# State-space tables from factors that are transposed once, complex products of three, and each batch's outputs directly in front of the next batch's products

## The chip, the core and the metric

The kernel runs on one core of a Trainium2 chip. The metric is the device time of one execution in microseconds (us); the time of a kernel is the median of its runs. The core has five engines that follow streams of instructions of their own: TensorE (PE) multiplies matrices and its weight loads (PEld) run beside the products, VectorE (DVE), ScalarE (ACT) and GpSimd (POOL) work on tiles element by element, and SyncE (SP) only issues DMA transfers. ACT and POOL can issue transfers too. Semaphores join the streams.

## What is computed

The input is a sequence of 1024 frames of 1024 channels in fp32. Layer 0 projects it to an S5 state-space branch and a retention branch, each with a SiLU gate, and maps both back; layer 1 is a gated convolution module. The change lies in the state-space branch, cut here to what matters:

```python
mag = exp(a_re * dt)                               # 64 groups x 64 states
lb  = mag * (cos(a_im * dt), sin(a_im * dt))       # complex decay of a step
bb  = coef(lb, a) * (b_re, b_im)                   # 64 groups x 64 states x 16 inputs
bu  = einsum('tbgh,gnh->tbgn', u, bb)              # inputs into the states
x   = associative_scan(lb, bu)                     # x[t] = lb * x[t-1] + bu[t]
y   = einsum(x_re, c_re) - einsum(x_im, c_im) + dsk * u
y   = gelu(y); y = y * sigmoid(y @ glu_w + glu_b)
```

## The kernel before

**Products of three.** A dense product takes three matmuls, high by high part, low by high, high by low (`mm3`, L276 to L278), each with 128x128 weights and 512 columns. A block of 128 output channels over the whole sequence is 2 halves x 8 x 3 = 48 matmuls.

**The first stage** is `layer0_front` (L337). It makes eight blocks `u` of the branch's input (`mm_u`; evacuated at L443, stored as `u_d` at L451), while DVE, ACT and POOL compute the state-space parameters (`s5_params`: powers `pr`, `pi` of the decay, phases `e1`, `e2`, and the factors `bbr`, `bbi`). Then come sixteen gate blocks (`mm_g`, nb 8 to 23), in pairs. During each pair one of eight *batches* B of the state-space layer is done, 128 channels each: 8 groups of 16, which are 4 pairs q of 2 groups with 128 states. Time is cut into 128 steps m of 8 frames j.

**A batch.** POOL makes three complex tables as outer products of the parameters (`s5_tables`, `outer`, six operations of 128x512 each): `Mr, Mi` (bb times the power j), the rotations `Tc, Ts`, and `W3` (c times the power j + 1). ACT makes `R8` (decay over 8 frames). `s5_states` then

- transposes Mr and Mi on PE in eight matmuls (`w2r`, `w2i`, L837), and ACT copies the two banks to `W2`;
- multiplies U, the batch's part of `u_d`, by W2 (`v`, L848), and DVE rotates and scans v into the states `S` (L856 to L876);
- makes the kernel matrix of a step: `kp` (L882, L883, eight matmuls of `cbr`, `cbni`, which are c set out in blocks by the host, with Mr and Mi), copied to `Kg` by ACT, with the skip `dd` added into its first 16 columns by DVE (L886), transposed on PE (`kt`, L888), copied to `Kt`, stored as one transfer into `k_d` (L892), read back as `Wd` in Toeplitz form (L895), and copied to `W1` (L897).

`s5_out(B)` makes the outputs of the batch: sixteen matmuls `y<-U,W` with W1 (L912) and thirty-two `y<-S,W` with W3 (L918), which ACT copies to `yb`, stored as `y_d` (L924). It is called for batch B - 1 after the first gate block of pair B.

**What sets the order.** Each engine runs its stream in order. A scheduler writes the streams from the program's dependencies with a timeline of its own and takes what comes earlier in the code first. It may set later independent instructions into a gap, which is why the same pieces stand at different distances in different batches. `issue_after` holds an instruction back behind another one, and `chained` keeps a list together. SP issues nearly all transfers, each in its place in SP's stream: the loads and stores of the batches, of the gates (`gs_d`, `gr_d`, L462) and of the *weight sums* (`weight_sums`, L244 to L254: rows `a` of another weight are loaded, added on DVE and stored as `ws`), which fill DVE and the transfers from nb 13 to nb 20. *Input sums* of the same kind follow in nb 9 to 12, held behind `last_kg`, the DVE operation at L886.

## Time and profile before

| | |
|---|---|
| median of 3 runs | 1179.47 us (1176.72 to 1180.49) |
| span of the profiled execution (its own time is not listed apart) | 1173.9 us |
| ACT busy | 545.1 us (46%), 821 instructions |
| transfers | 270.66 MB, mean 231 GB/s |
| Wd<-k_d, U<-u_d, y_d<-yb: 512 KB each, from issue to landing | 5.1, 4.6, 4.8 us |
| wf_g<-w_ab (weights of a gate block, 512 KB) | 5.4 us |
| first transpose w2 of batch 0 | 100.90 us after the span's start |

How such rows are read: a row of the timeline has the start in us, the length, the engine, the line of the code, the operation and its tiles (result <- operands), the shape, and the number of instructions put together in the row. `128*64 128x128` on PE is the shape of the weights and that of the moving operand. `SPq` is a transfer issued by SP. A square bracket tells how long the engine had been idle ahead of the row, and what ended that. A row of the waits has the engine and tile that waited, what it waited for, the sum in us, the count and the longest. A row of the windows has the window and its length, then for PE, DVE, ACT, POOL and PEld the busy time and the count of instructions, the granted clock, the share of the DMA engines that was busy, and GB/s.

### The profile page before, as it was taken

What the parts mean: (1) busy time and instruction counts of PE and PEld (TensorE: products, weight loads), DVE (VectorE), ACT (ScalarE), POOL (GpSimd) and SP (SyncE); (2) the same over time, 40 slices, a digit from 0 to 9 for tenths busy, and PEclk for the clock granted to TensorE, in tenths of its full rate; (3) what the DMA queues carried; (4) which work ended last, traced back from release to release, by engine and by line L of the source; (5) the groups of instructions that cost most, each with busy time, mean ns of one, the idle gap of its engine ahead of it and who ended that gap; (6) DMA issues with size and microseconds to landing.
All of it is one profiled execution on the core that took longest, in us unless ns stands there. A gap on an engine that the chain in (4) does not pass through costs nothing.

```text
span 1173.9 us, 17492 instructions
## 1 busy us (share of the span) xinstructions
PE 1161.3 (99%) x6150; PEld 965.5 (82%) x6150; DVE 910.5 (78%) x1507; ACT 545.1 (46%) x821; POOL 713.5 (61%) x507
## 2 busy tenths in 40 slices
PE   9999999999999999999999999999999999999997
PEld 7888888888888888887788888888888888888887
DVE  7875789999717475689777888479999999999643
ACT  7212343332226642123645544367756678544662
POOL 2049999888843245664444034348894689977742
PEclk9999999999999999999999999999999999999999
DMA  9353378778789765765988468965448553357863
GB/s 344 109 178 109 134 270 312 272 269 282 273 307 325 268 228 192 251 190 180 362 313 304 160 220 268 309 232 188 161 158 306 216 182 132 134 176 243 281 247 138
DMA packets 131192, 270.66 MB, mean 231 GB/s; under 512 B 12832, under 2 KB 41760, under 8 KB 130976
## 3 DMA queue, kind: packets, MB, share of 16 engines
q1 hardware_dynamic: 129952, 265.35, 66.5%
q10 hardware_dynamic: 1152, 4.19, 0.9%
q8 instruction: 48, 0.79, 0.3%
q14 instruction: 40, 0.33, 0.1%
HBM read 193.54 MB, written 71.76 MB: 226 GB/s over the span
## 4 chain that ended last, share of the span: by engine, by line
PE 91%; DMA 4%; DVE 2%; SPq 1%; ACT 1%; POOL 1%; issue 1%; DVEq 0%; POOLq 0%; ACTq 0%
PE mm_g L277 8%; PE mm_g L278 8%; PE mm_g L276 7%; PE mm_w L278 4%; PE mm_w L277 4%; PE mm_w L276 4%; PE mm_a L278 2%; PE mm_b L277 2%; PE mm_a L276 2%; PE mm_b L278 2%; PE mm_a L277 2%; PE mm_b L276 2%; PE mm_u L278 2%; PE mm_oc L278 2%; PE mm_u L277 2%; PE mm_oc L277 2%
## 5 line engine op out<-in xcount | busy, mean ns | idle before, releaser
L1461 DVE SCALAR_TENSOR_TENSOR cv<-u,convw,cv 128x512 f32<-128x512 f32 x358 | 244.7, 750 | 5.0 <-ACT cv L1447 3.5
L1441 POOL TENSOR_TENSOR tp<-tp,tp 128x512 f32<-128x512 f32 x104 | 138.9, 1338 | 28.7 <-ACT tp L1440 23.4
L278 PE MATMUL mm_g<-xh,wl_g 128*128 128x512 f32 x256 | 100.8, 394 | 0.0
L277 PE MATMUL mm_g<-xl,wh_g 128*128 128x512 f32 x256 | 100.7, 394 | 0.0
L276 PE MATMUL mm_g<-xh,wh_g 128*128 128x512 f32 x256 | 100.5, 393 | 0.0
L1440 ACT ACTIVATE tp<-u,convw 128x512 f32<-128x512 f32 x104 | 69.6, 713 | 9.6 <-POOL tp L1441 9.4
L277 PEld LDWEIGHTS mm_g<-xl,wh_g 128*128 128x128 f32 x256 | 48.1, 188 | 11.2 <-issue 1.6
L278 PEld LDWEIGHTS mm_g<-xh,wl_g 128*128 128x128 f32 x256 | 48.0, 188 | 10.5
L276 PEld LDWEIGHTS mm_g<-xh,wh_g 128*128 128x128 f32 x256 | 48.1, 188 | 9.6
L278 PE MATMUL mm_oc<-zh,wl_woc 128*128 128x512 f32 (+1 forms) x152 | 54.5, 360 | 0.2 <-DMA wl_woc<-lo_woc 0.2
L276 PE MATMUL mm_oc<-zh,wh_woc 128*128 128x512 f32 (+1 forms) x152 | 54.3, 362 | 0.0
L277 PE MATMUL mm_oc<-zl,wh_woc 128*128 128x512 f32 (+1 forms) x152 | 54.0, 357 | 0.0
L276 PE MATMUL mm_glu<-yh,wh_glu 128*128 128x512 f32 x128 | 50.0, 392 | 1.3 <-ACT sg L1250 1.3
L277 PE MATMUL mm_u<-xl,wh_u 128*128 128x512 f32 x128 | 50.1, 391 | 1.0 <-DVE xl L390 0.9
L276 PE MATMUL mm_g<-h1h,wh_cg 128*128 128x512 f32 x128 | 50.3, 393 | 0.0
L276 PE MATMUL mm_a<-h1h,wh_ca 128*128 128x512 f32 x128 | 50.3, 393 | 0.0
L278 PE MATMUL mm_b<-h1h,wl_cb 128*128 128x512 f32 x128 | 50.3, 393 | 0.0
L232 ACT CAST lh<-lf 128x512 fp32r<-128x512 f32 x32 | 19.5, 618 | 65.9 <-DMA lf<-w_c 59.3
L278 PE MATMUL mm_a<-h1h,wl_ca 128*128 128x512 f32 x128 | 50.0, 391 | 0.0
L277 PE MATMUL mm_glu<-yl,wh_glu 128*128 128x512 f32 x128 | 50.0, 392 | 0.0
L278 PE MATMUL mm_g<-h1h,wl_cg 128*128 128x512 f32 x128 | 49.9, 390 | 0.0
L277 PE MATMUL mm_g<-h1l,wh_cg 128*128 128x512 f32 x128 | 49.9, 390 | 0.0
(811 smaller groups left out, 3637.3 us busy)
## 6 DMA issues: line engine op xcount, KB each, us to landing
wf_g<-w_ab SPq DMA_DIRECT2D x16, 512.0 KB, 5.4
a<-w_out SPq DMA_DIRECT2D x32, 256.0 KB, 4.4
ws<-a SPq DMA_DIRECT2D x32, 256.0 KB, 4.8
lf<-w_c SPq DMA_DIRECT2D x32, 256.0 KB, 5.3
wf_p<-ws SPq DMA_DIRECT2D x16, 512.0 KB, 4.1
wf_cb<-w_c SPq DMA_DIRECT2D x16, 512.0 KB, 4.9
wf_ca<-w_c SPq DMA_DIRECT2D x16, 512.0 KB, 4.7
wl_cb<-lo_cb SPq DMA_DIRECT2D x16, 512.0 KB, 3.4
```

The costliest lines, as they stand in the source:

```text
L232: self.nc.scalar.copy(hi[:], f[:])
L276: nc.tensor.matmul(ps, wh[:, kb, :], xh, start=start, stop=False)
L277: nc.tensor.matmul(ps, wh[:, kb, :], xl, start=False, stop=False)
L278: self.last_mm = nc.tensor.matmul(ps, wl[:, kb, :], xh, start=False, stop=stop)
L1440: nc.scalar.mul(sk[:], u[:, k:k + HALF], cw[:, nb, k:k + 1])
L1441: gp.tensor_tensor(s0[:], s0[:], sk[:], op=ALU.add)
L1461: v.scalar_tensor_tensor(dst[:], *tap, accs_[i][:], op0=ALU.mult, op1=ALU.add)
```

## The change

Nothing changes in what the kernel computes. In the code:

- **Factors transposed once.** `bbr`, `bbi` are written with the inputs h ahead of q. After the first half of block u6, `s5_turned` transposes them and the powers in twelve matmuls (`turn_p`, `turn_br`, `turn_bi`); ACT copies the three banks and issues the stores to `pt_d` and `bt_d`, and copies the factors into `bblk`, set out in blocks of 32 columns. The host's `s5_cbr`, `s5_cbi` and their loads go, and the blocks u5 and u6 are now called ahead of the change of pools.
- **W2 without transposes.** Per batch, four transfers of 256 KB read `PT`, `BT` with repeats (from SP; for batch 0 from ACT), and POOL multiplies them in six operations directly into `W2`.
- **Complex products of three.** `Tc, Ts` and `W3` are made by `outer3`, five operations in place of six, from the sums and differences `psum`, `e1s`, `e2s`, `e1i` (now with e1r taken off), `cdif`, `csum`, which are made once.
- **The kernel matrix from W3.** W3 has nine times 16 columns; the first 16 are c itself, copied by ACT. kp is the product of W3 with `bblk`, which gives it in the transposed form, so that `kt` and `Kt` go. The skip is added on PE by four matmuls of the identity with 16 columns of `dd`, in place of the DVE operation. k_d is stored from ACT in eight transfers of runs of 64 bytes.
- **Order.** `s5_out(B - 1)` is called ahead of `s5_states(B)`, in front of the gate blocks. The input sums wait for the last write of S in place of `last_kg`. The stores of `y_d` and of the gates go from SP to ACT. The load of U is called in `s5_tables`, one gate block earlier. `tmpP`, `R8` have one buffer, `tmpV` two.

The first place is PE's stream around batch 3. Names carry the batch (`v_3`, `y_2`) and the scheduler's own number; `mm_g` are gate matmuls. Before, batch 3 is met in three pieces with gate matmuls between them:

```order
L837 MATMUL w2r_1928<-ident,Mr_1872 128x128 x4
L837 MATMUL w2i_1935<-ident,Mi_1873 128x128 x4
L276 MATMUL mm_g_0_2008<-xh_0_134,wh_g_1701 128x512
...
L848 MATMUL v_3_1942<-U_1926,W2r_1933 64x128 x8
L848 MATMUL v_3_1951<-U_1926,W2i_1940 64x128 x8
L882 MATMUL kp_1980<-Mr_1872,s_s_cbr 32x128
L883 MATMUL kp_1980<-Mi_1873,s_s_cbi 32x128
...
L888 MATMUL kt_1992<-ident,Kg_1989 128x128
L912 MATMUL y_2_2064<-U_1615,W_2_1688 128x128
L912 MATMUL y_2_2065<-U_1615,W_2_1688 128x128
...
L918 MATMUL y_2_2064<-S_1659,W_2_1577 128x128
L918 MATMUL y_2_2065<-S_1659,W_2_1577 128x128
```

After, the same place is one piece. Of the 48 matmuls y_2 the last four are shown:

```order
L973 MATMUL y_2_1972<-S_1720,W_2_1624 128x128
L973 MATMUL y_2_1973<-S_1720,W_2_1624 128x128
L973 MATMUL y_2_1972<-S_1720,W_2_1624 128x128
L973 MATMUL y_2_1973<-S_1720,W_2_1624 128x128
L904 MATMUL v_3_2001<-U_1944,W2r_1919 64x128 x8
L904 MATMUL v_3_2010<-U_1944,W2i_1920 64x128 x8
L937 MATMUL kp_2039<-W_3_1921,s_bblkr 32x128 x4
L939 MATMUL kp_2039<-s_s_dd,ident 32x16 x4
L940 MATMUL kp_2039<-W_3_1921,s_bblki 32x128 x4
L276 MATMUL mm_g_0_2073<-xh_0_134,wh_g_1768 128x512
L277 MATMUL mm_g_0_2073<-xl_0_135,wh_g_1768 128x512
```

The outputs y_2 have moved from behind the first gate block to the place right ahead of v_3; w2 and kt are gone, and the diagonal with `s_s_dd` stands between the two halves of kp. The batches 1 to 7 all look so, with 96 gate matmuls between one and the next. Batch 0 stands apart: its v in two parts and its kp in two lie among gate matmuls, and behind its last kp come 65 gate matmuls and then y_0.

The second place is PE's stream at the first half of block u6, which had only `mm_u` there before. The twelve transposes now stand between its two halves (`mm_u_0`, `mm_u_1`):

```order
L278 MATMUL mm_u_0_927<-xh_0_214,wl_u_803 128x512
L806 MATMUL turn_p<-ident,s_pr 128x128 x2
L806 MATMUL turn_p<-ident,s_pi 128x128 x2
L806 MATMUL turn_br<-ident,s_bbr 128x128 x4
L806 MATMUL turn_bi<-ident,s_bbi 128x128 x4
L276 MATMUL mm_u_1_986<-xh_1_142,wh_u_802 128x512
L277 MATMUL mm_u_1_986<-xl_1_143,wh_u_802 128x512
```

They are 72 matmuls `mm_u` ahead of the first gate matmul. Nothing of them is in the batches any more.

The third place is SP's stream between the outputs of batch 2 and the W1 of batch 3. Before (weight sums `a`, `ws` all around):

```order
L892 DMA k_d<-Kt_1994 128x128
L830 DMA U_2225<-u_d 128x1024
L895 DMA Wd_1997<-k_d 128x8x128
L462 DMA gs_d<-gt_2007 128x1024
L254 DMA ws_0_1914<-a_1_2095 128x512
L265 DMA wf_g_2599<-w_ab 128x1024
```

After, at the load of the same Wd (the number after its name is the scheduler's):

```order
L868 DMA PTr_2505<-ptr 128x1x512
L871 DMA BTi_2508<-bti 128x1x512
L244 DMA a_2_2252<-w_out 128x512
...
L868 DMA PTi_2506<-pti 128x1x512
L871 DMA BTr_2507<-btr 128x1x512
L950 DMA Wd_2062<-k_d 128x8x128
L254 DMA ws_0_1959<-a_1_2130 128x512
```

The store of k_d and that of the gate have left SP, and four loads PT, BT of batch 5 stand a few rows ahead of the load of Wd of batch 3. The stores are now in ACT's stream, with SiLUs (`gt`), a weight cast (`wh_g`), `R` and the two copies of c (`W`) between them:

```order
L977 COPY yb_1971<-y_2_1972 128x4x128
L977 COPY yb_1971<-y_2_1973 128x4x128
L878 COPY W_4_2218<-s_s_cr 128x4x16
L878 COPY W_4_2218<-s_s_ci 128x4x16
L979 DMA y_d<-yb_1971 128x1024
L944 COPY Kg_2052<-kp_2039 128x128
L947 DMA k_d<-Kg_2052 16x8x16 x8
L886 ACTIVATE R_4_2243<-s_s_m_480,s_r_614 128x128 x4
L462 ACTIVATE gt_2072<-gt_2072 128x512
L267 CAST wh_g_2145<-wf_g_2144 128x1024
L462 ACTIVATE gt_2072<-gt_2072 128x512
L465 DMA gs_d<-gt_2072 128x1024
```

In ACT's stream of batch 3 there stand now, between the copy of yb and that of W1, the store of y_d, the copy of Kg, eight stores of k_d and one of a gate.

The diff, cut to its core:

```diff
...
@@ -443,6 +443,9 @@
                 self.u_evac[nb] = nc.vector.tensor_tensor(
                     ut[:, ::-1, h * 64:(h + 1) * 64], ps[:].rearrange("p (m j) -> p j m", j=8),
                     r.rearrange("p (m j) -> p j m", j=8), op=ALU.mult)
+                if (nb, h) == (6, 0):
+                    with tc.issue_after(self.last_mm.ins):
+                        self.s5_turned(ev)
...
-            nc.sync.dma_start(dst[k * P:(k + 1) * P], gt[:])
+            nc.scalar.dma_start(dst[k * P:(k + 1) * P], gt[:])
...
+        for nb in (5, 6):
+            u_block(nb)
         early.close()
         sums = self.pool("sums", 1, stack=st)
         self.s5 = self.pool("s5w", 1, stack=st)
-        for nb in range(5, 8):
-            u_block(nb)
+        u_block(7)
         self.s5_tab, self.s5_back, self.s5_last = {}, {}, None
         self.s5_tables(0)
         for nb in range(8, 24):
             B = (nb - 8) // 2
             if nb % 2 == 0:
+                if B:
+                    self.s5_out(B - 1)
                 self.s5_states(B)
                 if nb in (10, 12):
-                    with self.tc.issue_after(self.last_kg.ins):
+                    with self.tc.issue_after(self.last_s.ins):
...
-            if nb % 2 == 0 and B:
-                self.s5_out(B - 1)
...
-        self.cbr, self.cbni = load("s5_cbr", (NP, 32)), load("s5_cbi", (NP, 32))
+        self.bblk = [sp.tile([P, NP, 32], F32, name=f"s5_bblk{c}") for c in "ri"]
+        for b in self.bblk:
+            nc.gpsimd.memset(b[:], 0.0)
...
+        self.psum = t((9, NP), keep="s5_psum")
+        tt(self.psum[:], pr_[:], pi_[:], ALU.add)
+        self.cdif, self.csum = t((NP, 16), keep="s5_cdif"), t((NP, 16), keep="s5_csum")
...
+        self.e2s = t((8, NP), keep="s5_e2s")
+        self.e1s = t((17, NP), keep="s5_e1s")
+        tt(self.e2s[:], e2r[:], e2i[:], ALU.add)
+        tt(self.e1s[:], e1r[:], e1i[:], ALU.add)
+        self.last_phase = tt(e1i[:], e1i[:], e1r[:], ALU.subtract)
...
-        self.bbr, self.bbi = t((NP, 16), keep="s5_bbr"), t((NP, 16), keep="s5_bbi")
+        self.bbr, self.bbi = (tp.tile([P, 16, NP], F32, name=f"s5_bb{c}") for c in "ri")
...
+        tt(self.cdif[:], self.cr[:], self.nci[:], ALU.add, gp)
+        tt(self.csum[:], self.cr[:], self.nci[:], ALU.subtract, gp)
...
-        tt(self.bbr[:], x1[0], x1[1], ALU.subtract, gp)
-        tt(self.bbi[:], x1[2], x1[3], ALU.add, gp)
+        tt(self.bbr[:].rearrange("p h q -> p q h"), x1[0], x1[1], ALU.subtract, gp)
+        tt(self.bbi[:].rearrange("p h q -> p q h"), x1[2], x1[3], ALU.add, gp)
+    def s5_turned(self, tp):
+        nc = self.nc
+        self.pt_d = [self.dram.tile([8, 32, P], F32, name=f"pt{c}") for c in "ri"]
+        self.bt_d = [self.dram.tile([16, 32, P], F32, name=f"bt{c}") for c in "ri"]
+        def turn(name, srcs, dsts):
+            ps = self.bank(f"turn_{name}")
+            for i, src in enumerate(srcs):
+                nc.tensor.transpose(ps[:, i * P:(i + 1) * P], src, self.ident[:])
+            t = tp.tile([P, 8, P], F32, name=f"turned_{name}", tag="xin", bufs=8)[:, :4, :]
+            self.last_turn = nc.scalar.copy(t.rearrange("p i n -> p (i n)"), ps[:])
+            n = len(srcs) // len(dsts)
+            for i, dst in enumerate(dsts):
+                nc.scalar.dma_start(dst.rearrange("(i p) n -> p i n", p=P), t[:, i * n:(i + 1) * n, :])
+        fl = lambda t: t.rearrange("p a b -> p (a b)")
+        cols = lambda t, n: [fl(t)[:, i * P:(i + 1) * P] for i in range(n)]
+        rows = lambda d: d[:].rearrange("a b n -> (a b) n")
+        turn("p", cols(self.pr[:, 0:8, :], 2) + cols(self.pi[:, 0:8, :], 2), [rows(d) for d in self.pt_d])
+        for c, b in zip("ri", (self.bbr, self.bbi)):
+            turn(f"b{c}", cols(b[:], 4), [rows(self.bt_d["ri".index(c)])])
+        for blk, b in zip(self.bblk, (self.bbr, self.bbi)):
+            for g in range(2):
+                r = slice(64 * g, 64 * g + 64)
+                with self.tc.issue_after(self.last_turn.ins):
+                    nc.scalar.copy(blk[r, :, 16 * g:16 * g + 16], b[r].rearrange("p h q -> p q h"))
...
+    def outer3(self, B, o_r, o_i, k1, k2, k3, view, op_i):
+        gp = self.nc.gpsimd
+        t = self.big(f"o_{B}", "tmpP", 1)
+        yield gp.tensor_tensor(view(t[:]), *k1, op=ALU.mult)
+        yield gp.tensor_tensor(view(o_r), *k3, op=ALU.mult)
+        yield gp.tensor_tensor(o_r, t[:], o_r, op=ALU.subtract)
+        yield gp.tensor_tensor(view(o_i), *k2, op=ALU.mult)
+        yield gp.tensor_tensor(o_i, o_i, t[:], op=op_i)
...
-        made = [self.outer(B, Mr[:], Mi[:], bj(self.bbr), bj(self.bbi), pj(self.pr), pj(self.pi), vm)]
...
+        made = [self.outer3(B, Tc[:], Ts[:], (ea(self.e2s), eb(self.e1[0])), (ea(self.e2[0]), eb(self.e1[1])),
+                            (ea(self.e2[1]), eb(self.e1s)), vt, ALU.add)]
+        PT, BT = ([self.big(f"{n}{c}_{B}", n + c, 1) for c in "ri"] for n in ("PT", "BT"))
+        queue = nc.sync if B else nc.scalar
+        for t, d in zip(PT, self.pt_d):
+            queue.dma_start(t[:], bass.AP(tensor=d.tensor, offset=d.offset + qs.start * P,
+                                          ap=[[32 * P, 8], [0, 16], [1, 4 * P]]))
+        for t, d in zip(BT, self.bt_d):
+            queue.dma_start(t[:], bass.AP(tensor=d.tensor, offset=d.offset + qs.start * P,
+                                          ap=[[0, 8], [32 * P, 16], [1, 4 * P]]))
+        W2 = [self.big(f"W2{c}_{B}", f"W2{c}", 1) for c in "ri"]
+        made.append(self.outer(B, W2[0][:], W2[1][:], BT[0][:], BT[1][:], PT[0][:], PT[1][:], lambda ap: ap))
+        W3 = w.tile([P, 2, 4, 9 * 16], F32, name=f"W3_{B}", tag="W3", bufs=2)
+        for c, t in enumerate((self.cr, self.nci)):
+            nc.scalar.copy(W3[:, c, :, 0:16], t[:, qs, :])
+        made.append(self.outer3(B, W3[:, 0, :, 16:], W3[:, 1, :, 16:], (pj(self.psum), bj(self.cr)),
+                                (pj(self.pr), bj(self.cdif)), (pj(self.pi), bj(self.csum)), vm, ALU.subtract))
         self.s5_last = self.chained(chain(*made), self.s5_last)
-        R8 = self.big(f"R8_{B}", "R8", 2)
+        U = w.tile([P, 8, P], F32, name=f"U_{B}", tag="U", bufs=2)
+        nc.sync.dma_start(U[:], self.u_d[B].rearrange("j h g m -> (j h) g m"))
...
-            for q in range(4):
-                nc.tensor.transpose(ps[:, q * P:(q + 1) * P], M[:, q, :], self.ident[:])
-            t = self.big(f"W2{nm}_{B}", f"W2{nm}", 1)
-            nc.scalar.copy(t[:].rearrange("p q n -> p (q n)"), ps[:])
...
+        self.last_s = v.tensor_tensor(c1(S[:, 1]), c0(zi), c0(t3), op=ALU.add)
...
-            nc.tensor.matmul(o, self.cbr[:, q0 + q, :], Mr[:, q, :], start=True, stop=False)
-            nc.tensor.matmul(o, self.cbni[:, q0 + q, :], Mi[:, q, :], start=False, stop=True)
+        kp, made = self.bank(f"kp_{B}"), []
+        rows = [slice(q * 32, (q + 1) * 32) for q in range(4)]
+        made += [nc.tensor.matmul(kp[r, :P], self.bblk[0][:, q0 + q, :], W3[:, 0, q, :P], start=True, stop=False)
+                 for q, r in enumerate(rows)]
+        made += [nc.tensor.matmul(kp[r, :16], self.ident[:, r], self.dd[:, B, :], start=False, stop=False) for r in rows]
+        made += [nc.tensor.matmul(kp[r, :P], self.bblk[1][:, q0 + q, :], W3[:, 1, q, :P], start=False, stop=True)
+                 for q, r in enumerate(rows)]
+        self.chained(made)
         Kg = w.tile([P, P], F32, name=f"Kg_{B}", tag="Kg", bufs=1)
         nc.scalar.copy(Kg[:], kp[:, :P])
-        self.last_kg = v.tensor_tensor(Kg[:, :16], Kg[:, :16], self.dd[:, B, :], op=ALU.add)
-        kp = self.bank(f"kt_{B}")
-        nc.tensor.transpose(kp[:, :P], Kg[:], self.ident[:])
-        Kt = w.tile([P, P], F32, name=f"Kt_{B}", tag="Kg", bufs=1)
-        nc.scalar.copy(Kt[:], kp[:, :P])
-        nc.sync.dma_start(self.k_d[B, 112:], Kt[:])
+        kd = self.k_d[B, 112:].rearrange("(j i) (g o) -> g i j o", j=8, g=8)
+        for g in range(8):
+            nc.scalar.dma_start(kd[g], Kg[16 * g:16 * g + 16].rearrange("p (j o) -> p j o", j=8))
...
-        nc.sync.dma_start(self.y_d[B].rearrange("i h g m -> (i h) g m"), yb[:])
+        nc.scalar.dma_start(self.y_d[B].rearrange("i h g m -> (i h) g m"), yb[:])
...
```

More of the change, by code (lines that the diff above doesn't have):

```diff
@@ L825, in s5_states @@
         q0 = 4 * B
[L826 to L840 removed]
+        U, W2, W3, Tc, Ts, R8 = self.s5_tab.pop(B)
         V = []
```

40 lines of the change are left out of this document (9 added, 31 removed).

## The prediction

> **What bounds the kernel now.** The page first: which engine is full, and at what clock.
>
> ```profile
> span 1173.9 us, 17492 instructions
> ...
> PE 1161.3 (99%) x6150; PEld 965.5 (82%) x6150; DVE 910.5 (78%) x1507; ACT 545.1 (46%) x821; POOL 713.5 (61%) x507
> ...
> PEclk9999999999999999999999999999999999999999
> ```
>
> TensorE is busy for 1161.3 of 1173.9 us, at the full granted clock in every slice. "Busy" alone could hide matmuls that wait, so the next view is the list of what PE waited for. It has eight rows, 6.1 us in all; the first and the last are:
>
> ```profile
> PE mm_glu L276 <- ACT sg L1250: 1.3, 1, 1.3
> ...
> PE mm_oc L278 <- DMA wl_woc<-lo_woc: 0.2, 1, 0.2
> ```
>
> None of the eight names a tile of the state-space stage, where the whole change lies. There the span is the sum of PE's own work: a PE instruction taken out of it shortens the kernel by its step on PE, and work on any other engine counts only if PE comes to wait for it. So the third view is PE's timeline through one batch (batch 3), read by starts, since the lengths of neighbours overlap.
>
> ```profile
> 155.95 0.60 PE L837 MATMUL w2r<-ident,Mr 128*128 128x128 f32 x4
> ...
> 185.46 0.60 PE L837 MATMUL w2r<-ident,Mr 128*128 128x128 f32 x4
> 185.89 0.60 PE L837 MATMUL w2i<-ident,Mi 128*128 128x128 f32 x4
> 186.25 0.47 PE L276 MATMUL mm_g<-xh,wh_g 128*128 128x512 f32 x1
> ...
> 191.45 1.09 PE L848 MATMUL v<-U,W2r 128*64 128x128 f32 x16
> 192.38 1.04 PE L848 MATMUL v<-U,W2i 128*64 128x128 f32 x16
> 193.35 0.45 PE L882 MATMUL kp<-Mr,s_s_cbr 128*32 128x128 f32 x8
> 193.59 0.42 PE L883 MATMUL kp<-Mi,s_s_cbi 128*32 128x128 f32 x8
> 193.94 0.50 PE L277 MATMUL mm_g<-xl,wh_g 128*128 128x512 f32 x1
> 194.28 0.39 PE L278 MATMUL mm_g<-xh,wl_g 128*128 128x512 f32 x1
> ...
> 200.43 0.27 PE L888 MATMUL kt<-ident,Kg 128*128 128x128 f32 x1
> 200.54 1.95 PE L912 MATMUL y<-U,W 128*128 128x128 f32 x16
> 202.42 2.06 PE L918 MATMUL y<-S,W 64*128 64x128 f32 x32
> 204.40 0.50 PE L278 MATMUL mm_g<-xh,wl_g 128*128 128x512 f32 x1
> ...
> 205.67 0.39 PE L277 MATMUL mm_g<-xl,wh_g 128*128 128x512 f32 x1
> ...
> 210.65 0.39 PE L278 MATMUL mm_g<-xh,wl_g 128*128 128x512 f32 x1
> ```
>
> A batch lasts 185.46 - 155.95 = 29.51 us. Its 96 gate matmuls step by (210.65 - 205.67) / 22 = 0.226 us, 21.73 together. The small products take, from start to start: the eight transposes w2 0.79 (0.099 each), v 1.90, kp 0.59 (16 passes of 0.037, two for each of the 8 matmuls), kt 0.11, y 3.86: 7.25. The 0.53 left is the seams where the stream changes between gate and small products (0.34 instead of 0.226 behind kp, for one); there are three interruptions a batch, so 0.18 for each.
>
> **The change on PE.** *Removed* in each batch: w2 0.79 and kt 0.11. *Added* in each batch: the four diagonal matmuls in kp. The kernel matrix now takes 12 matmuls, 24 passes, against 16. No pass with 16 moving columns is in the trace; it loads 32 columns of weights as the passes of kp do, so 0.037 is the nearest row, and kp becomes 24 x 0.037 = 0.88, 0.29 more. Bounds for those 64 passes of the whole kernel: nothing at all (2.4 us better), or the 0.117 of a pass of y with 128 columns of weights (1.88 / 16), which is 64 x 0.080 = 5.1 us worse. Below nothing I see no reason: the other passes are the same in number, at a step already far under that of y. Work per batch: 0.79 + 0.11 - 0.29 = 0.61, in eight batches **4.9 us**.
>
> *Moved*: y of the batch before, v and kp now stand in one block. Before there are three interruptions in each batch and one for the last y, 25; after, batch 0 has four (its v in two parts, its kp in two), batches 1 to 7 one each, the last y one, the turned factors one: 13. Twelve seams at 0.18 are **2.2 us**. Bounds: nothing (that the 0.53 is a slower step spread over the matmuls and stays), or twice that. *Added once*: 12 transposes of factors at 0.099, **1.2 us**. Sum on PE: 4.9 + 2.2 - 1.2 = **5.9 us**.
>
> **What has to stay hidden.** Every other edit costs nothing as long as PE is not made to wait. Three covers count.
>
> The turned factors. They follow the first half of u6, 72 matmuls ahead of the first gate block, which starts after the first w2:
>
> ```profile
> 68.29 0.44 DVE L607 TENSOR_TENSOR s_e1i<-s5t,s5t 128x256 f32<-128x256 f32 x1
> ...
> 81.64 1.29 POOL L607 TENSOR_TENSOR s_bbi<-s5bb 128x512 f32<-128x512 f32 x1
> ...
> 100.90 0.60 PE L837 MATMUL w2r<-ident,Mr 128*128 128x128 f32 x4
> ```
>
> That is 100.90 - 72 x 0.226 = 84.6 us. The last factor is ready at 82.93 now; three new DVE sums (288, 544, 544 wide, with 256 at 0.44 about 2 us) come ahead of it and a scaling of 128x1024 goes, and POOL now writes it with a stride. So 84 to 85: level with its reader. I allow 0.5 us of waiting on PE. Behind it ACT issues eight transfers and POOL makes W2 of batch 0; v of batch 0 stands 26 gate matmuls later than the block's start, about 24 us after the turn, which covers two trips through memory and eleven POOL operations.
>
> The way from kp to the finished W1. It was free to take most of a batch; now y of a batch stands 96 gate matmuls, 21.7 us, behind its kp, and in batch 0 only 65, 14.7 us.
>
> ```profile
> 203.27 0.33 SPq L892 DMA_DIRECT2D k_d<-Kt  x1
> 204.81 0.37 SPq L895 DMA_DIRECT2D Wd<-k_d  x1
> ...
> 210.34 1.05 ACT L897 COPY W<-Wd 128x1024 f32<-128x1024 f32 x1 [5.75 <-DMA Wd<-k_d]
> ...
> 212.71 0.67 DVE L875 TENSOR_TENSOR S<-v,d 128x508 f32<-128x508 f32 x1
> ```
>
> From the store's issue to W1 is 211.39 - 203.27 = 8.1 us. Eight stores from ACT in place of one add 7 x 0.33 = 2.3, the Kg copy about 0.5: 11 us. On SP the load of Wd now stands behind the four new loads for a later batch, which wait until POOL is done with the old tiles, six operations of some 1.3 us after v; then W1 is there about 8 + 1.5 + 5.5 + 1 = 16 us after v. Cover: 5 us in the batches, some 2 us in batch 0, where a SiLU that waits for DVE stands ahead of the stores. I allow 0.5 us there. What queues behind a late store on ACT are the SiLUs, the weight casts and the copy of yb; PE would see the y products late first.
>
> The states S. They must be written 23.6 us after v (96 matmuls and the first half of y). Before, the last write comes 212.71 + 0.67 - 193.35 = 20 us after v with a set of weight sums ahead of it; after, it stands ahead of the weight sums, so some 10 us earlier. POOL drops from 18 to 16 operations in a batch, DVE loses the small sum into Kg; neither is on the path.
>
> So 5.9 - 1.0 = **4.9 us less**. The profiled execution has a span of 1173.9 us; its own time is not listed apart, and the median of the runs, 1179.47, is 5.6 more, which I carry over. Span 1169.0, time **1174.6 us**. About 0.3%, 3.5 us, is what a measurement of this kernel can tell from no change.
>
> **Rivals.** *W1 late, or the diagonal dear.* If y waits for W1 0.5 us in each of seven batches, 3.5 us go and 1.4 remain: 1178.1. With the diagonal at its upper bound 0.8 remain: 1178.7. For it: 64-byte pieces in the new stores, the shared queue semaphores that an issue can wait for, the order on SP. Against: the 5 us above.
>
> *The transfers become the bound: slower.* Each batch reads 1.05 MB more (four tiles of 256 KB).
>
> ```profile
> 0.00:29.35 29.35, 27.14 (x129) 22.25 (x130) 20.96 (x30) 22.58 (x32) 7.51 (x10) 1.00 0.93 344
> 185.00:215.00 30.00, 30.00 (x205) 25.06 (x204) 28.76 (x32) 9.80 (x19) 27.83 (x20) 1.00 0.86 303
> 245.00:275.00 30.00, 30.00 (x207) 25.19 (x206) 27.83 (x32) 9.69 (x19) 26.24 (x20) 1.00 0.81 276
> ```
>
> The last two columns are the DMA engines' busy share and GB/s. At 303 / 0.86 = 352 GB/s the extra is 3.0 us a batch. The fullest batch has 0.86 x 29.5 + 3.0 = 28.4 us of it, four more about 0.81 x 29.5 + 3.0 = 26.9, in batches of 29.5 - 1.0 = 28.5. If 0.86 were all that this stage's mix can use, these become 33.0 and 31.3: 4.5 + 4 x 2.8 = 15.7 us lost against 5.9 won, DVE late with its weight sums and PE behind it, 9.8 us **slower**, 1189.3. It decides where the usable share falls under 26.9 / 28.5 = 0.94. Against: 0.93 was held for the first 29 us; loads of the sums run two sets ahead. The Trainium skill, "Trainium Kernel Development and Optimization", Key Constraints, says that transfers issued from SP and from ACT run on the same 16 engines and that a second issuer saves issue time alone. By it the stores moved to ACT bring no room and the shares stand as worked out; if they brought room, this rival would fall away. No row here tells the two apart.
>
> *Transposes cost their length.*
>
> ```profile
> L837 PE MATMUL w2r<-ident,Mr x32: 269/272/273, 100.9 to 303.8; 128*128 128x128 f32 x32
> ```
>
> At 0.272 instead of 0.099 for 72 - 12 = 60 transposes the gain is 10.4 us larger: 1164.2. Against it: eight of them fit into 0.79 us. The Trainium skill, "TensorE: Matmul & The Clock Gate", Part 4: PE-mode transpose, gives about 275 ns for one in a kernel; the length agrees, the steps do not.
>
> **Chances.** Forecast (3.5 to 8.3 us less) 0.60; W1 or diagonal 0.25; transfers 0.11; lengths 0.04. Faster 0.64, same 0.25, slower 0.11. The range goes from 1170.5 (diagonal and waits at nothing, 8.3 less, and a little over) to 1181.0, past the no-gain cases; left out are the slower rival and the lengths.
>
> **What would show it.** The batch on PE near 28.5 us, w2 and kt gone, kp at 0.9, one interruption. Wrong if y products, v or the turned factors head PE's list of waits; if the DMA share passes 0.93 and DVE waits for weight-sum loads; if the batch is 28.5 and the span is not shorter, then the gain was given back behind 350 us.

## The result, and the profile after

| | before | changed |
|---|---|---|
| median of four runs | 1178.11 us (1176.72 to 1180.49) | 1207.22 us (1202.63 to 1213.95) |
| ratio | | **1.025**, 95% interval 1.0215 to 1.0286 |
| span of the profiled execution | 1173.9 us | 1204.8 us |

The runs before are the three of the first table and one more. The change makes the kernel 29 us slower. The forecast was 4.9 us faster, and the time lies far outside the range of 1170.5 to 1181.0. The page of the changed kernel, its first lines and the clock:

```profile
span 1204.8 us, 17593 instructions
...
PE 1162.2 (96%) x6154; PEld 965.4 (80%) x6154; DVE 901.6 (75%) x1502; ACT 542.2 (45%) x820; POOL 693.4 (58%) x495
...
PEclk9999998999999999999999999999999999999999
```

TensorE's busy time is the same (1162.2 against 1161.3), but the span holds 31 us more. So PE waits, and one slice shows a lower clock; matmuls at the lower clock take longer, which fills up the busy time that the change saves. What PE waited for, with the sum, the count and the longest wait:

```profile
PE y L967 <- ACT W L952: 22.3, 4, 9.7
...
PE kp L940 <- POOL W L845: 1.9, 2, 1.2
...
PE v L904 <- POOL W2i L835: 1.2, 1, 1.2
...
PE v L904 <- POOL W2r L835: 0.7, 1, 0.7
...
PE turn_bi L806 <- POOL s_bbi L611: 0.6, 1, 0.6
```

The output products wait for W1 in four batches, 22.3 us; the waits named kp, v and turn_bi are of the first batches and come to 4.4 us. None of these rows was there before. PE's timeline shows the first long wait, for the outputs of batch 2:

```profile
190.01 0.39 PE L278 MATMUL mm_g<-xh,wl_g 128*128 128x512 f32 x1
200.14 3.71 PE L967 MATMUL y<-U,W 128*128 128x128 f32 x16 [9.74 <-ACT W L952]
203.78 2.06 PE L973 MATMUL y<-S,W 64*128 64x128 f32 x32
...
207.66 0.43 PE L937 MATMUL kp<-W,s_bblkr 128*32 128x128 f32 x8
207.90 0.23 PE L939 MATMUL kp<-s_s_dd,ident 128*32 128x16 f32 x8
207.96 0.40 PE L940 MATMUL kp<-W,s_bblki 128*32 128x128 f32 x8
208.30 0.50 PE L276 MATMUL mm_g<-xh,wh_g 128*128 128x512 f32 x1
...
234.95 3.38 PE L967 MATMUL y<-U,W 128*128 128x128 f32 x16 [4.55 <-ACT W L952]
```

A wait is dearer than its length. The sixteen `y<-U,W` behind it take 203.78 - 200.14 = 3.64 us, where they took 1.88 before. The windows around it give the granted clock (third from the end of a row), the DMA share and GB/s:

```profile
190.00:194.00 4.00, 0.40 (x2) 0.00 (x0) 3.34 (x2) 1.16 (x2) 3.84 (x4) 0.93 0.41 130
194.00:200.00 6.00, 0.00 (x0) 0.00 (x0) 5.12 (x5) 0.96 (x2) 5.84 (x5) 0.50 0.96 288
200.00:204.00 4.00, 3.86 (x20) 3.71 (x22) 1.15 (x2) 2.09 (x4) 1.85 (x2) 0.54 1.04 348
```

PE stopped at 190.4. A clock of 0.93 over the first four us is a fall to 0.5 at about 193.4, and 0.54 from 200 to 204, with 1.00 from there on, is a return at about 203.7: half clock from 3.0 us into the wait until 3.5 us after it, 10.3 us in all. Windows of 1 us around the other three waits show half clock from 234.4 to 237.8 (4.0 us into the wait of 4.55 us until 2.8 us after it), from 299.2 to 306.0 (4.5 us into the wait of 6.62 us until 4.7 us after it), and none at the wait of 1.34 us. The Trainium skill, "TensorE: Matmul & The Clock Gate", Part 1, names one window of 3.4 us for both changes; the three stretches of 10.3, 3.4 and 6.8 us agree, as whole multiples of it. At half clock the sixteen matmuls took twice as long, so half of the time at half clock behind a wait is lost: 1.8, 1.4 and 2.4 us on top of the three waits, 5.5 us in all. A whole window without work is not needed for it: b3 below has half clock behind waits of 1.9 to 2.8 us.

The last `y` ends 27.2 us later than before; the other 3.7 us of the span come behind it. Most of the 27.2 us can be placed: 26.7 us of waits and 5.5 us of half clock, less the 5.9 us that PE was to save, are 26.3. The last product before, and after:

```profile
345.75 2.06 PE L918 MATMUL y<-S,W 64*128 64x128 f32 x32
```

```profile
372.99 2.06 PE L973 MATMUL y<-S,W 64*128 64x128 f32 x32
```

Now the way of the W1 that was late at 234.95. Its kernel matrix left PE at 208.3. ACT's timeline from there (`ACTq` is a transfer that ACT issues):

```profile
210.35 0.34 ACTq L979 DMA_DIRECT2D y_d<-yb  x1
210.88 0.27 ACT L944 COPY Kg<-kp 128x128 f32<-128x128 f32 x1 [2.96 <-DMA gs_d<-gt]
214.79 7.38 ACTq L947 DMA_DIRECT2D k_d<-Kg  x8
222.22 1.28 ACT L886 ACTIVATE R<-s_s_m,s_r 128x128 f32<-128x128 f32 x4 [11.07 <-DVE v L929]
...
233.85 1.04 ACT L952 COPY W<-Wd 128x1024 f32<-128x1024 f32 x1 [8.35 <-DMA Wd<-k_d]
```

And SP's, which loads Wd:

```profile
227.79 0.38 SPq L950 DMA_DIRECT2D Wd<-k_d  x1
```

From the end of kp to W1 it is 26.6 us: 2.6 until ACT has issued y_d and copies Kg; 3.9 from there to the first store; 7.4 for the eight stores; 5.6 from the last of them to the issue of Wd; 6.1 for its load; 1.0 for the copy. The eight issues take about 0.33 us each when nothing holds them. Here they are held, and ACT's list of waits says what stood behind them:

```profile
ACT W L952 <- DMA Wd<-k_d: 52.0, 8, 9.7
...
ACT R L886 <- DMA k_d<-Kg: 37.3, 4, 12.1
...
ACT gt L462 <- DMA k_d<-Kg: 18.6, 2, 12.8
```

R and the SiLUs `gt` stand behind the stores in ACT's stream: 55.9 us. (The R of batch 3, at 222.22, is not in this sum: its row names a DVE operation that ended at 221.90, just ahead of the end of the last store's issue at 222.17.) The program shows why an issue can wait. Each transfer from SP or ACT counts on one of eight semaphores that the two share, and an issue waits until the transfer that had its semaphore before has landed (the program's rows for the stores of batch 3, with the names of the semaphores):

```
L947 DMA k_d<-Kg_2052 16x8x16 [waits DMAHW5_49,Activation_49]
L947 DMA k_d<-Kg_2052 16x8x16 [waits DMAHW6_49]
L947 DMA k_d<-Kg_2052 16x8x16 [waits DMAHW7_49]
L947 DMA k_d<-Kg_2052 16x8x16 [waits DMAHW0_49]
```

The trace has the same: each of the eight issues waits on the semaphore that its own store then counts on. The transfers waited for can be SP's as well as ACT's own (e5 below shows Kg behind SP's load of U), and they land late. The windows of the busy stretch, after:

```profile
190.00:220.00 30.00, 20.26 (x157) 17.20 (x156) 21.09 (x21) 5.83 (x11) 24.11 (x18) 0.83 0.91 316
220.00:250.00 30.00, 25.45 (x182) 21.47 (x181) 24.59 (x32) 7.95 (x16) 18.36 (x14) 0.94 0.92 298
```

The DMA share is 0.91 and 0.92 where PE waits most. So two things could have made W1 late: the new stores on ACT (theory A below), or the new loads that keep the transfers full (theory B, later L). The order that leaves W1 only 96 matmuls is a third (theory C).

### The profile page after: what moved, and what is told of

It reads as the page before. It is cut to its first block, busy times and chain, and to the rows that moved or that the text cites. A ratio compares the mean times of both kernels' runs of the same rounds, so it can differ in the third digit from the quotient of the medians.

```text
span 1204.8 us, 17593 instructions
## 1 busy us (share of the span) xinstructions
PE 1162.2 (96%) x6154; PEld 965.4 (80%) x6154; DVE 901.6 (75%) x1502; ACT 542.2 (45%) x820; POOL 693.4 (58%) x495
## 4 chain that ended last, share of the span: by engine, by line
PE 62%; DVE 2%; DMA 2%; issue 2%; ACT 0%; SPq 0%; POOL 0%; DVEq 0%; ACTq 0%
PE mm_w L276 4%; PE mm_w L277 4%; PE mm_w L278 4%; PE mm_oc L276 2%; PE mm_oc L277 2%; PE mm_oc L278 2%; PE mm_a L278 2%; PE mm_g L276 2%; PE mm_g L277 2%; PE mm_a L276 2%; PE mm_b L276 2%; PE mm_a L277 2%; PE mm_b L277 2%; PE mm_g L278 2%; PE mm_b L278 2%; PE mm_glu L276 2%
## 5 line engine op out<-in xcount | busy, mean ns | idle before, releaser
L1495 ACT ACTIVATE tp<-u,convw 128x512 f32<-128x512 f32 x104 | 69.7, 713 | 11.8 <-POOL tp L1496 11.6
L268 DVE TENSOR_TENSOR wl_g<-wf_g,wh_g 128x1024 fp32r<-128x1024 f32 x16 | 26.4, 1648 | 33.5 <-ACT wh_g L267 33.5
L276 PE MATMUL mm_u<-xh,wh_u 128*128 128x512 f32 x128 | 49.5, 397 | 0.4 <-ACT wh_u L267 0.3
```

The source lines that it names most:

```text
L268: lo[i].tensor_tensor(wl[:].rearrange(fl)[:, c], wf[:, c], h.bitcast(F32), op=ALU.subtract)
L276: nc.tensor.matmul(ps, wh[:, kb, :], xh, start=start, stop=False)
L1495: nc.scalar.mul(sk[:], u[:, k:k + HALF], cw[:, nb, k:k + 1])
```

## Experiments

All times are medians; the ratio to the kernel before stands with its 95% interval, against runs of it on the same chip (its median lay between 1177.16 and 1177.78 us).

### First round: one suspect out at a time

**e1: one store.**

```diff
-        for g in range(8):
-            nc.scalar.dma_start(kd[g], Kg[16 * g:16 * g + 16].rearrange("p (j o) -> p j o", j=8))
+        nc.scalar.dma_start(self.k_d[B, 112:], Kg[:])
```

> Kg goes to k_d in one transfer from ACT in place of eight, as it lies in the tile; the values in k_d so stand at other places than the kernel matrix needs. All else as in the changed kernel. Theory A (the eight small stores make W1 late: issued over 7.4 to 8.1 us on ACT because each waits for an earlier transfer's semaphore, landed 4.8 to 5.5 us after the last issue): W1 comes about 10 us earlier in each batch, more than the longest wait of 9.7 us, the four waits of y for W1 (22.3 us) go, and the time is 1176 to 1181. Theory B (the loads of PT and BT hold up the transfer queues): the one store and the load of Wd still land late, half of the waits stay, 10 us or more, and the time is above 1188. Theory C (the new order leaves too little room whatever the stores do): as the changed kernel, above 1200.

Measured 1205.91 us, 1.0245 (1.0212 to 1.0278). The waits for W1 fell to 14.9 us, but the time did not: theory A alone falls.

**e2: loads in 16 steps.**

```diff
-ap=[[32 * P, 8], [0, 16], [1, 4 * P]]
+ap=[[0, 16], [32 * P, 8], [1, 4 * P]]
...
-ap=[[0, 8], [32 * P, 16], [1, 4 * P]]
+ap=[[32 * P, 16], [0, 8], [1, 4 * P]]
```

> The loads of PT and BT of 256 KB are read with a slowest dimension of 16 steps in place of 8, the same bytes in another order of the partitions; the factors so stand at other partitions than W2 needs. Stores and order as in the changed kernel. In its trace the 512 packets of batch 0's four loads ran mostly at most 8 at a time over 10.4 us. Theory B (these loads use 8 of the 16 DMA engines and hold up what is queued behind them on those): the eight stores and Wd land earlier, PE's waits for W1 fall from 22.3 us to under 8, the time is below 1190. Theory A (the number of stores is what counts): the waits stay above 15 us, the time at 1200 to 1208. Theory C: no change either.

Measured 1199.87 us, 1.0202 (1.0162 to 1.0242): 7 us better by the medians, though the intervals of this run and of the change overlap, and waits for W1 still 19.2 us. That is the waits of theory A, with a time just under its range. What the steps do can be seen where hardly any other transfer runs, behind the loads issued from 111.77 to 114.47 us in the change and from 108.58 to 111.13 us here. The changed kernel:

```profile
116.00:118.00 2.00, 2.00 (x10) 1.65 (x9) 2.00 (x5) 0.00 (x0) 1.92 (x3) 1.00 0.52 158
118.00:120.00 2.00, 2.00 (x23) 1.44 (x23) 2.00 (x4) 0.84 (x1) 1.92 (x2) 1.00 0.49 175
120.00:122.00 2.00, 1.96 (x15) 1.18 (x14) 2.00 (x3) 1.01 (x3) 1.92 (x3) 1.00 0.15 54
```

This run:

```profile
112.00:114.00 2.00, 2.00 (x17) 1.57 (x12) 1.42 (x3) 0.00 (x0) 1.92 (x3) 1.00 1.02 188
114.00:116.00 2.00, 2.00 (x11) 1.57 (x9) 2.00 (x4) 0.00 (x0) 1.92 (x3) 1.00 0.95 147
116.00:118.00 2.00, 2.00 (x30) 1.13 (x28) 2.00 (x4) 1.19 (x2) 1.92 (x2) 1.00 0.26 90
```

A share of 0.5 in place of about 1: with a slowest dimension of 8 steps the loads occupy half of the DMA engines. The Trainium skill, "DMA: Bandwidth & Descriptors", Rules for kernel authors, says that a slowest dimension of size c below 16 confines a transfer to at most c of the 16 engines; the shares agree. What it does not lead one to expect: on 16 engines the four loads are hardly sooner (the share falls some 8 us behind the first issue in both), and they bring 147 to 188 GB/s at a share of 1, where the busy stretch of before had 303 at 0.86.

**e3: outputs later.**

```diff
-                if B:
-                    self.s5_out(B - 1)
                 self.s5_states(B)
...
             gate_block(nb, self.wnext(f"g{nb}"), self.gs_d if nb < 16 else self.gr_d)
+            if nb % 2 == 0 and B:
+                self.s5_out(B - 1)
```

> The outputs of batch B - 1 are called behind the even gate block again, as before the change, so that they stand 144 matmuls (32.6 us) behind their kernel matrix in place of 96 (21.7 us); the factors, products of three, stores and loads are those of the changed kernel. Theories A and C: the chain from kp to W1 keeps its 22 to 32 us and is covered but for batch 2 (31.7 us from the end of kp to W1) at most, the waits for W1 go, and what is left is PE's own saving less batch 0: 1174 to 1180. Theory B in its strong form (the transfers are the bound of the stage): the time stays above 1190, with waits that have moved to other tiles.

Measured 1205.90 us, 1.0242 (1.0227 to 1.0258). The waits for W1 went, and others came in their place:

```profile
PE v L904 <- DMA U<-u_d: 13.0, 3, 7.8
```

So the order alone does not save it, against theories A and C: the time is above 1190 and the waits have moved, as theory B has it. The tile that is late now is U, which SP loads behind the loads of PT and BT and the load of Wd.

**e4: the large stores on SP again.**

```diff
-nc.scalar.dma_start(self.y_d[B].rearrange("i h g m -> (i h) g m"), yb[:])
+nc.sync.dma_start(self.y_d[B].rearrange("i h g m -> (i h) g m"), yb[:])
...
-            nc.scalar.dma_start(dst[k * P:(k + 1) * P], gt[:])
+            nc.sync.dma_start(dst[k * P:(k + 1) * P], gt[:])
```

> The stores of y_d and of the gates (512 KB each) are issued from SP again, so that ACT issues only the eight stores of k_d. Order and loads as in the changed kernel. If it is ACT's stream that delays the chain (the store of y_d stands ahead of Kg and waited until 210.35 us in batch 3, and the small stores queue behind it): Kg follows kp within 1 us, W1 comes 3 to 6 us earlier, the waits fall to about 5 to 12 us, 1185 to 1196. Theory A (the eight stores themselves): as the changed kernel, at most 3 us less per batch, above 1196. Theory B: no change, above 1200.

Measured 1204.99 us, 1.0236 (1.0220 to 1.0252), waits for W1 20.8 us. Kg followed kp closely in seven of the eight batches, and W1 was no earlier (in batch 3 its copy starts at 233.83 us, in the change at 233.85).

### Second round: the loads out

**e5: PT and BT loaded once.**

```diff
-        PT, BT = ([self.big(f"{n}{c}_{B}", n + c, 1) for c in "ri"] for n in ("PT", "BT"))
+        if B == 0:
+            self.factors = [[self.big(f"{n}{c}_{B}", n + c, 1) for c in "ri"] for n in ("PT", "BT")]
+        PT, BT = self.factors
...
+        if B == 0:
+            (the four loads)
```

> PT and BT are loaded for batch 0 alone and used by all batches, so batches 1 to 7 have the factors of batch 0; all else as in the changed kernel, the eight stores and the new order too. Theory L (the four loads, 1.05 MB a batch, are what the transfer engines can't carry beside the rest: share 0.92 from 190 to 250 us, with at most 2 of the engines at work in 4% of the time against 9% before): the share falls to 0.85 or less there, the waits for W1 fall from 22.3 us to under 4, the time is 1172 to 1180. Theory A (the eight stores on ACT) or C (the order): waits for W1 above 12 us, time above 1190.

Measured 1193.78 us, 1.0125 (1.0089 to 1.0160): 13 us of the 29. The time is that of theories A and C, and the waits for W1 fell to 6.9 us, between what they and theory L allow. ACT in this run, in batch 3:

```profile
206.69 0.27 ACT L947 COPY Kg<-kp 128x128 f32<-128x128 f32 x1 [5.94 <-DMA U<-u_d]
206.99 6.87 ACTq L950 DMA_DIRECT2D k_d<-Kg  x8
213.90 1.28 ACT L889 ACTIVATE R<-s_s_m,s_r 128x128 f32<-128x128 f32 x4 [6.95 <-DMA k_d<-Kg]
```

Without the loads ACT is still held: 5.9 us ahead of Kg, where the transfer that came last is SP's load of U, and 6.9 us in the stores.

**e6: a quarter of the loads.**

```diff
+        nq = 1 if B else 4
-            queue.dma_start(t[:], ... ap=[[32 * P, 8], [0, 16], [1, 4 * P]]))
+            queue.dma_start(t[:, 0:nq], ... ap=[[32 * P, 8], [0, 16], [1, nq * P]]))
```

> Batches 1 to 7 load a quarter of PT and BT only (one pair of four, 64 KB in place of 256 KB for each of the four loads, pieces of 512 bytes in place of 2048); the other three pairs keep the factors of batch 0. The same 28 issues in the same places of SP's stream, with the same waits for POOL ahead of them. If the bytes count (theory L): a quarter of the loss or somewhat more, 1178 to 1186, waits for W1 under 7 us. If it is the issues themselves (four more places a batch in the rotation of semaphores, and SP held by a wait for POOL): as the changed kernel, above 1195, waits above 12 us.

Measured 1194.91 us, 1.0135 (1.0104 to 1.0166), within the noise of e5, with 7.8 us of waits for W1: outside both cases, of which the first counted on far less without loads than e5 shows. The 28 issues and their waits for POOL cost about nothing beside the stores; it is what the loads carry.

**e7: W2 from PE's transposes again.** Mr and Mi by `outer` as before, eight transposes and two copies; no turned factors, no loads.

```diff
-        PT, BT = ([self.big(f"{n}{c}_{B}", n + c, 1) for c in "ri"] for n in ("PT", "BT"))
...
-        made.append(self.outer(B, W2[0][:], W2[1][:], BT[0][:], BT[1][:], PT[0][:], PT[1][:], lambda ap: ap))
+        Mr, Mi = self.big(f"Mr_{B}", "Mr", 1), self.big(f"Mi_{B}", "Mi", 1)
+        made.append(self.outer(B, Mr[:], Mi[:], bh(self.bbr), bh(self.bbi), p0(self.pr), p0(self.pi), vm))
```

> The factors are not transposed; POOL makes Mr and Mi in six operations as before the change and PE transposes them in eight matmuls a batch, and ACT copies W2. Kept from the change: products of three for Tc, Ts and W3, kp from W3 with the skip on PE, the eight stores from ACT, the stores of y_d and gates from ACT, the new order. Theory L: no loads, so no waits for W1 to speak of; PE's saving is 4.7 us less the transposes' 6.3 and with the 1.2 for turning the factors back, so about the time of before: 1175 to 1182. Theory A: the eight stores are still there, above 1190.

Measured 1193.24 us, 1.0127 (1.0107 to 1.0147). A miss for theory L, in favour of A: the stores on ACT and the order are enough for 16 us without any load.

**b1: the order alone, in the kernel before.**

```diff
+                if B:
+                    self.s5_out(B - 1)
                 self.s5_states(B)
...
-            if nb % 2 == 0 and B:
-                self.s5_out(B - 1)
```

> The kernel before with one edit: the outputs of batch B - 1 are called ahead of the states of batch B. Theory L: the transfers are those of before and the chain to W1 takes the 17 to 18 us of before at most against a cover of 70 to 100 matmuls, so within 0.4% of before, 1174 to 1181. Theory C (the new order is what costs): waits for W1 appear, above 1185.

Measured 1186.26 us, 1.0066 (1.0046 to 1.0086). Both theories miss: hardly a wait for W1 (0.6 us), and still 9 us. About half of it is one stall in batch 3, 3.5 us of waiting and 1.6 us of half clock behind it, on PE and on DVE:

```profile
PE kt L888 <- DVE Kg L886: 3.5, 1, 3.5
```

```profile
207.80 1.23 DVE L250 TENSOR_TENSOR a<-a,a 128x512 f32<-128x512 f32 x1 [3.92 <-DMA a<-w_out]
...
214.99 1.23 DVE L886 TENSOR_TENSOR Kg<-Kg,s_s_dd 128x16 f32<-128x16 f32 x1
```

A weight sum ahead of the rotation of v waits 3.9 us for its load, and the small sum into Kg comes behind it. Most of the rest appears behind 350 us and wasn't followed.

### Third round: several suspects out together

**e8: e5 and e1 together** (no loads, one store).

> As the run without the loads of PT and BT behind batch 0 (1193.78 us), and Kg stored in one transfer too (its values at other places of k_d). There the waits for W1 were 6.9 us and ACT stood for 57 us behind its own stores of Kg. Theory P (two causes that hide one another: with the loads the transfers are full whatever the stores do; without them the issues on ACT, which wait for the landing of earlier transfers, are what is late): ACT's wait behind the stores of Kg falls by 40 us or more, waits for W1 under 3 us, 1180 to 1188. Theory L (loads alone): nothing more to win, 1190 to 1196.

Measured 1187.64 us, 1.0086 (1.0056 to 1.0115). The one store, which gave 1 us beside the loads, gives 6 without them by the medians (the intervals overlap); waits for W1 are 0.9 us, and ACT's waits behind its stores of Kg fall from 56.8 us to 3.2. Theory P.

**e9: e5 and e3 together** (no loads, outputs later).

> As the run without the loads, with the outputs behind the even gate block again; the eight stores stay. Theory P: the chain from kp to W1 of 22 to 28 us is covered by 144 matmuls (32.6 us), no wait for W1, but ACT is still held by its issues, so SiLUs and weight casts stay late: 1178 to 1188. Theory L: 1190 to 1196, the order changes nothing.

Measured 1184.54 us, 1.0063 (1.0044 to 1.0082), no wait for W1: the later order, too, gives 9 us where it gave 1.

**e12: e5, e1 and e4 together** (no loads, one store, large stores on SP).

> Without the loads, with one store of Kg, and with the stores of y_d and of the gates issued from SP as before the change: ACT issues one small transfer a batch. The new order and all products are those of the change. Theory P: now ACT is not held, the transfers are those of before, and what is left is PE's saving: 1172 to 1179. If the new order costs by itself (b1, the order alone, was 1186.26): 1182 to 1190.

Measured 1183.83 us, 1.0060 (1.0041 to 1.0079): not theory P, but the second case. 6.7 of the 29 us are left. This run has the order of the change, and where nothing waits it shows what a batch takes then; the outputs of batch 5 and of batch 6 start 28.30 us apart:

```profile
279.65 1.95 PE L968 MATMUL y<-U,W 128*128 128x128 f32 x16
```

```profile
307.95 1.95 PE L968 MATMUL y<-U,W 128*128 128x128 f32 x16
```

**e13: e2, e1 and e4 together** (loads in 16 steps).

> All the loads of PT and BT, but with a slowest dimension of 16 steps (factors at other partitions), one store of Kg, stores of y_d and gates from SP. Bytes as in the changed kernel. Theory of bytes (the stage can't carry 1.05 MB more a batch however they are issued): above 1192. If issue, engines and order on ACT are all that costs: below 1185.

Measured 1201.46 us, 1.0207 (1.0191 to 1.0223), as the theory of bytes has it. Against e12 the loads alone make 18 us, also on all engines: W1 is late again (11.6 us of waits), at a DMA share of 0.90 and 0.93 from 190 to 250 us.

### Fourth round: one suspect in at a time, in the kernel before

**b2: loads added**, in 8 steps and, in a second kernel, in 16 steps. PE's order is that of before. To make room, both kernels also have the fewer buffers of `tmpP`, `R8` and `tmpV` that the change has.

```diff
+        if B < 7:
+            d = self.A["w_out"][0]
+            with self.tc.issue_after(uload.ins):
+                for i, ap in enumerate((p8, p8, b8, b8)):
+                    t = self.big(f"X{i}_{B}", f"X{i}", 1)
+                    nc.sync.dma_start(t[:], bass.AP(tensor=d.tensor, offset=..., ap=ap))
```

> The kernel before with four loads of 256 KB added behind the load of U in batches 0 to 6, from a weight, with the strides of the change's loads (slowest dimension 8 steps), into tiles that nothing reads; PE's order is that of before, and three scratch tags have one buffer or two less to make room. Theory of bytes (the stage can't carry 1.05 MB more a batch): waits on PE appear for weights or W1 and the time is 10 us or more above before, 1187 to 1200. If the loads hurt in the changed kernel only because its order has little room: under 1183.

> The same with a slowest dimension of 16 steps. If a load of 8 steps keeps half of the DMA engines busy twice as long, this one costs about half of the run with 8 steps; if only bytes count, the same as that run within 3 us.

Measured 1197.47 us, 1.0172 (1.0152 to 1.0192) in 8 steps, and 1182.29 us, 1.0044 (1.0027 to 1.0061) in 16. The loads (with the fewer buffers) make a loss of 20 us; spread over all engines, the same bytes make one of 4.5, less than the half that was expected. So the fewer buffers cost 4.5 us at most. In 8 steps PE waits in two places:

```profile
PE kt L894 <- DVE Kg L892: 7.7, 1, 7.7
PE v L854 <- ACT W2r L845: 5.5, 1, 5.5
```

In 16 steps it waits in one of them:

```profile
PE kt L894 <- DVE Kg L892: 3.6, 1, 3.6
```

With 8 steps the tile is late in both places because its engine first waits for another load: DVE 7.4 us for the rows `a` of a weight sum ahead of Kg, and ACT 10.1 us for `xa` ahead of the copy of W2r.

**b5: the stores on ACT**, eight for Kt, and y_d and the gates; **b3: the eight stores alone.**

```diff
-        nc.sync.dma_start(self.k_d[B, 112:], Kt[:])
+        kd = self.k_d[B, 112:].rearrange("(j i) (g o) -> g i j o", j=8, g=8)
+        for g in range(8):
+            nc.scalar.dma_start(kd[g], Kt[16 * g:16 * g + 16].rearrange("p (j o) -> p j o", j=8))
```

> The kernel before with Kt stored in eight pieces of 16 partitions from ACT with runs of 64 bytes (values at other places of k_d), and the stores of y_d and of the gates from ACT. No extra loads, order of before. If ACT's issues are a cause by themselves: ACT stands 40 us or more behind its own transfers, and the time is 3 to 10 us above before, 1181 to 1188. If they hurt only beside the loads: under 1180.

> The kernel before with one edit: Kt stored in eight pieces from ACT with runs of 64 bytes (values at other places of k_d). If the eight stores make the 18 us of b5: 1188 to 1197. If the stores of y_d and of the gates on ACT do: under 1182.

Measured 1195.41 us, 1.0145 (1.0120 to 1.0171) for b5, which is dearer than either of its cases, and 1196.24 us, 1.0155 (1.0130 to 1.0179) for b3. The eight stores alone make 18 to 19 us, with no new load and in the old order; the large stores on ACT add nothing. Before's order leaves W1 room enough, and here another tile is the victim, which ACT also copies. PE's waits in b3:

```profile
PE v L848 <- ACT W2r L839: 9.6, 6, 2.6
...
PE v L848 <- ACT W2i L839: 2.8, 1, 2.8
```

ACT's timeline shows why W2r is late:

```profile
209.75 5.72 ACTq L894 DMA_DIRECT2D k_d<-Kt  x8
...
229.26 1.04 ACT L899 COPY W<-Wd 128x1024 f32<-128x1024 f32 x1 [6.53 <-DMA Wd<-k_d]
230.21 0.58 ACT L839 COPY W2r<-w2r 128x512 f32<-128x512 f32 x1
```

From the issue of the first store to W1 it is 230.30 - 209.75 = 20.6 us, where it was 8.1 before. W1 is late here as it is in the change; its copy stands ahead of that of W2r in ACT's stream, and v waits for W2r. Behind four of these waits, of 1.9 to 2.8 us, the clock is 0.5 for 3.4 us each, which costs some 6.6 us more: 12.4 and 6.6 are 19.0 us.

**e14: all four suspects out** (no loads, one store, large stores on SP, outputs later).

> The changed kernel without the loads behind batch 0, with one store of Kg, the stores of y_d and gates from SP, and the outputs behind the even gate block. What is left of the change: factors turned once and W2 from POOL, products of three, kp from W3 with the skip on PE. If the four suspects are all: 1172 to 1179. If batch 0 (factors through memory, v and kp waiting for POOL) has a price of its own, about 7 us, and nothing else: 1179 to 1185.

Measured 1183.09 us, 1.0050 (1.0033 to 1.0067), within the second case. What is left is the start:

```profile
PE v L907 <- POOL W2i L835: 2.5, 2, 1.3
...
PE kp L943 <- POOL W L845: 1.9, 1, 1.9
PE kp L940 <- POOL W L843: 1.2, 1, 1.2
```

v and kp of the first batches wait 5.6 us for POOL's W2 and W3, in pieces, and behind the waits of kp the clock is 0.5 until 173.6 us, some 2.9 us more. From batch 3 on nothing waits: the outputs of batch 3 and of batch 4 start

```profile
238.91 1.95 PE L968 MATMUL y<-U,W 128*128 128x128 f32 x16
```

```profile
267.41 1.95 PE L968 MATMUL y<-U,W 128*128 128x128 f32 x16
```

28.50 us apart, where a batch took 29.51 before, and 28.30 in e12, in whose order y, v and kp are one piece.

**e15: e13 with the outputs later** (loads in 16 steps, one store, large stores on SP, outputs later).

> As e13 (loads in 16 steps, one store of Kg, stores of y_d and gates from SP; 1201.46 us) with the outputs behind the even gate block. If the loads are dear in e13 because y stands only 96 matmuls behind its kernel matrix: e14's 1183.09 and the 4.5 us that such loads cost before the change, 1184 to 1191. If the loads hurt by another way (SP held for POOL, late loads of U): above 1195.

Measured 1190.19 us, 1.0103 (1.0088 to 1.0118), inside the first case: with room behind kp the loads in 16 steps cost 7 us (against e14), with the short order 18 (e13 against e12). W1 is not waited for; the longest wait is one of 4.8 us of v, for POOL.

No kernel was below the time of before; the nearest with the change's products, e14, was 5.3 us above it and left work out.

## Why the prediction was wrong

**PE's own work was right but for one term.** In the order of the change a batch was to take 28.5 us (29.51 - 0.61 - 2 x 0.18 = 28.54); it takes 28.30 where nothing waits (e12). The diagonal was sized too high: kp takes 208.30 - 207.66 = 0.64 us, not 0.88, since its eight passes with 16 columns take 0.06 together. That is the 0.24 us by which the batch is shorter. A seam was sized rightly: e14, which has one more in a batch, takes 28.50, so one is worth 0.20 us against the forecast 0.18. The turned factors were level with their reader as forecast (a wait of 0.57 us).

**The step that failed is the way from kp to W1.** It was put at 16 us behind v, with 5 us of cover to spare and 0.5 us of waiting for the whole stage. It measures 26.6 us behind kp in batch 3, which is 29.1 us behind v (205.76 to 234.89), and four waits of 22.3 us, with 5.5 us of half clock behind three of them. Two terms of it were mis-sized:

- *"Eight stores from ACT in place of one add 7 x 0.33 = 2.3."* That is the price of an issue that nothing holds. They took 7.4 us in batch 3, and 6.5 us had gone by before the first. The shared semaphores were named in the first rival, as an argument only. b3 shows the price in a kernel with nothing else of the change: 18.9 us. Such a store delays all that stands behind it on ACT; whether the wait, the number, the pieces of 64 bytes or the move from SP to ACT weighs most wasn't separated (e1 and e8 change the first three at once, b3 all four). One store can be held too: in e12, with no loads, Kg is copied at 199.47, its store is issued at 206.55, Wd at 213.00, and W1 is done at 218.70, only 2.5 us ahead of its reader.
- *The loads were priced as bytes*, 3.0 us a batch at 352 GB/s over 16 engines. At batch 0 their share of 0.5 shows them on half of the engines, for some 8 us; on 16 engines they take as long. b2 shows the price: 19.7 us, of which 15 go when the slowest dimension has 16 steps. Why the half that is occupied makes PE wait so much longer, though the loads themselves land no sooner on 16 engines, was seen at the two tiles only (ACT and DVE late by their waits for other loads), not traced to single transfers.

**The new order was counted as a gain of twelve seams.** The seams are gained, but the order alone loses 8.7 us (b1), by a stall of another kind and by time behind 350 us. That no price was put on it was a gap: cover for DVE's work was checked for S, not for the sums ahead of it.

**The start** was allowed 0.5 us for the turn and nothing for POOL's tables; kp, v and turn_bi waited 4.4 us there in the changed kernel. In e14 the waits and the half clock there come to 8.5 us, more than the 5.3 us that this run is above the time of before.

**The rivals.** The first had the place right, and a size of 3.5 us for W1 that was six times too small. The second had the sign. Its turning point, a usable share under 0.94, is not what the runs show: PE waits at shares of 0.90 to 0.93 over 30 us (the change and e13), but e9 has 0.93 from 220 to 250 us with PE busy throughout. Its sum, 1189.3, knew the bytes alone, and neither the stores nor the engines that a load uses. The parts don't add: loads 19.7, stores 18.9 and order 8.7 us alone make 47, together 29. They hide one another, as e3 shows, where the wait moves from W1 to U: PE waits for the tile that is latest, and with one cause away the next sets the time. That is why four single removals gave 1 to 7 us and looked like misses.

## What to carry to other kernels

Price a transfer by what its issue waits for and by how many DMA engines its shape uses, not by the 0.33 us of the issue or by its bytes: eight small stores a batch on an engine with other work, or seven batches of loads whose slowest dimension has 8 steps, cost some 19 us each here in a kernel that was otherwise all but unchanged. When single removals give little, put each suspect alone into the old kernel; that showed at once what taking parts out of the new one hid.
